# Compressed latents of an attention layer: four passes in the order query 0, key 0, key 1, query 1 in place of query 0, query 1, key 0, key 1

## The chip, the cores and the metric

The kernel runs on one NeuronCore of one Trainium2 chip. TensorE (PE) does the matrix products and the transposes, VectorE (DVE) and ScalarE (ACT) the elementwise work, GpSimd (POOL) a little, and SyncE (SP) issues most of the loads. The metric is the device time of one execution in microseconds (us): 2163.89 us, the median of three runs (2162.13 to 2165.8).

## What is computed

A two-layer encoder over one sequence of 1024 tokens with width 1024, all in float32. Layer 0 is a short gated convolution and a squared-ReLU MLP. Layer 1 is latent attention with 8 heads and a second MLP. The change is at the seam between layer 0 and the attention of layer 1. There the residual stream is normalised, and two modulated versions of it are made: `h`, from which the queries come, and `hkv`, from which the keys and values come. Each is projected to a narrow latent, the latent is normalised, and the key side gives a rotary key as well:

```python
kv_a = hkv @ kv_a_w                                   # 1024 -> 256 + 64
c_kv = rmsnorm(kv_a[..., :KV_LORA], kv_a_norm_g)      # 256 wide
k_pe = apply_rope(kv_a[..., KV_LORA:], cos, sin)      # rotary key, 64 wide
kv = (c_kv @ kv_b_w).reshape(B, S, N_HEADS, QK_NOPE + V_HEAD)
...
q = (rmsnorm(h @ q_a_w[j], q_a_norm_g[j]) @ q_b_w[j])  # 1024 -> 384 -> heads
```

Then come scores, a softmax under a block-causal mask of chunks of 64 tokens, and the weighted values.

## The kernel before

**Products in three parts.** A float32 product is taken as three products of parts: an operand is rounded to a high part by a copy on ACT, and DVE subtracts it from the original, which leaves the low part. `mm` (L154 to L156) then adds low weights by high data, high weights by low data and high by high into the same sum. `up_split` and `split_w` (L159, L160) do this for weights: `uphi` and `uplo` are the parts of one block of 128 weight columns (128x1024). There are three buffers of each, so a fourth block has to wait until the first has been used.

**Tokens in halves.** The seam works on row tiles (`y`) of 128 tokens; tiles 0 to 3 are half 0 and tiles 4 to 7 half 1. A latent pass takes one half (512 tokens) through all weight blocks: three blocks for the query (384 columns), two for the key (256) and one for the rotary key. One block is 8 steps over the width (`KD`) of three products, 24 products of 128x512.

**The operand of a pass.** `h_steps` makes it, in 8 steps: PE transposes the four row tiles of the half into one PSUM tile (L420), ACT scales and shifts it with the modulation into `tt` (L423), DVE casts the high part (L428) and subtracts the low part (L429). There are two such PSUM tiles (`tp`) and two `tt`. The steps are given to a pass as `steps`, and are written between its products. Two operand buffers are there: `hs[0]` (made in the down projection before, with the query's modulation "1m") and `hs[1]`.

**The end of the layer before.** `Seam.tile` closes a row tile: ACT sums its squares (L271) and takes the root (L273), DVE scales it (L327) and adds the residual (L328), ACT stores it and sums the squares of the new residual, and `flush` scales it for the next layer (L311, into `y`). For tile 7, the last, `flush` is called inside `first_latents`, the function that does the products of query 0. Its operand's last step but one comes after tile 4 and its last after tile 5.

**Order of the latents before.** Query 0 (`first_latents`, with the steps of query 1's operand in its third block), query 1 (with the steps of key 0's operand), key 0 and rotary key 0 (with those of key 1), key 1, rotary key 1. `latent` (L1165 to L1187) evicts each block (L1177), squares it (L1178), sums the squares over the partitions by a product with ones (L1181), takes the root (L1182) and the reciprocal (L1183), scales (L1185) and splits (L1186, L1187) into `qaT` or `ckT`. `rotated` (L1189 to L1197) turns the rotary sums with four copies of 32 rows on ACT (L1194). The split weights of q_a stay for both query passes. Then the weights of the first head are split, and the attention begins, with queries, rotary queries and keys of half 1, then of half 0; the values of the first head lie between the first scores.

**What sets the order on an engine.** The program writes the operations; a scheduler of the tile framework merges them into one list for each engine, keeping dependences; the written order binds it only in `pinned` blocks. Inside a pinned block, and from one pinned block to what comes before, an engine keeps the order in which the operations were written. Each engine works through its list in order.

## Time and profile before

| | |
|---|---|
| median of three runs | 2163.89 us (2162.13 to 2165.8) |
| the profiled execution | 2163.67 us |
| its span, first to last instruction | 2161.9 us |
| mean granted TensorE clock | 0.99 |
| PE busy | 2066.3 us (96%) |
| DVE busy | 1541.7 us (71%) |
| ACT busy | 1082.9 us (50%) |
| moved by DMA | 344.47 MB, mean 159 GB/s |

All times inside the execution are counted from the start of its span. A row of a timeline gives the start, the length, the engine, the line of the kernel before, the operation with its output and inputs and their shapes, and in brackets how long the engine stood idle before it and what released it. Neighbours on one engine overlap by some tenths of a us, so that in a dense row of operations the distance of the starts is the cost. Groups give the number, the busy time, the mean length in ns and the idle time before them.

### The profile page before, as it was taken

Reading aid. Unit: us, or ns where it says so; the run is one execution under the profiler, and the core shown is the slowest. Engines: PE = TensorE matmul, PEld = TensorE weight load, DVE = VectorE, ACT = ScalarE, POOL = GpSimd, SP = SyncE. Lnnn points to the kernel's source line nnn. Section 1 sums busy time; section 2 is a strip of 40 time slices with the busy share of each in tenths; the row PEclk is TensorE's granted clock in tenths of the full one; section 3 lists DMA queues with packets and bytes.
Section 4 is the critical chain, followed back from the end, with each engine's and each line's share of the span. In section 5 each row is a group of like instructions: output and inputs, shape, how many; then the busy total and the mean of one; then the engine's idle time right before and its main releaser. Section 6 shows DMA issues by size and latency. Waiting matters only on the chain.

```text
span 2161.9 us, 25072 instructions
## 1 busy us (share of the span) xinstructions
PE 2066.3 (96%) x9438; PEld 1690.4 (78%) x9438; DVE 1541.7 (71%) x2087; ACT 1082.9 (50%) x1533; POOL 5.3 (0%) x13
## 2 busy tenths in 40 slices
PE   4999999899999999999899999989899999999998
PEld 3788878678888788888677888878678888788886
DVE  6777876876765679877688887765875665566577
ACT  4533354745554444455665655564744454544443
POOL 0000000000000000000000000000000000000000
PEclk9999999999999999999999999999999999999999
DMA  7344464254653889656214231053254653774255
GB/s 224 111 146 146 136 207 142 82 180 161 191 183 128 287 291 324 202 171 207 69 60 127 90 100 35 25 169 127 65 187 156 216 180 126 267 248 163 95 175 173
DMA packets 251023, 344.47 MB, mean 159 GB/s; under 512 B 19253, under 2 KB 142482, under 8 KB 250902
## 3 DMA queue, kind: packets, MB, share of 16 engines
q1 hardware_dynamic: 208408, 252.50, 37.2%
q10 hardware_dynamic: 42494, 90.38, 11.3%
q8 instruction: 74, 1.21, 0.2%
q14 instruction: 47, 0.39, 0.1%
HBM read 258.94 MB, written 83.89 MB: 159 GB/s over the span
## 4 chain that ended last, share of the span: by engine, by line
PE 78%; DVE 11%; ACT 6%; DMA 3%; issue 2%; ACTq 0%; SPq 0%; DVEq 0%
PE one L156 42%; PE mm L156 20%; PE tp L156 7%; PE big L156 4%; PE big L1340 2%; ACT junk L271 2%; DVE y L327 1%; PE tp L1366 1%; DVE raw L328 1%; ACT z L1194 1%; DMA aw<-in_ada_w_dram 1%; DMA raw<-hd 1%; PE tp L420 1%; DVE acc L186 1%; DVE av L892 1%
## 5 line engine op out<-in xcount | busy, mean ns | idle before, releaser
L156 PE MATMUL one<-slot,uphi 128*128 128x512 f32 x1224 | 377.6, 389 | 0.0
L156 PEld LDWEIGHTS one<-slot,uphi 128*128 128x128 f32 x1224 | 230.1, 188 | 48.0 <-issue 0.5
L156 PE MATMUL one<-ring,ring 128*128 128x512 f32 x1152 | 262.9, 389 | 2.3 <-DVE ring L160 2.3
L160 DVE TENSOR_TENSOR uplo<-raw,uphi 128x1024 fp32r<-128x1024 f32 x127 | 153.2, 1221 | 143.1 <-ACT uphi L159 143.1
L156 PEld LDWEIGHTS one<-ring,ring 128*128 128x128 f32 x1152 | 215.9, 188 | 48.3 <-ACT ring L159 3.1
L156 PE MATMUL one<-slot,uplo 128*128 128x512 f32 x612 | 240.5, 393 | 8.2 <-DVE y L515 3.8
L160 DVE TENSOR_TENSOR ring<-raw,ring 128x1024 fp32r<-128x1024 f32 x144 | 174.1, 1219 | 53.8 <-ACT ring L159 53.3
L159 ACT ACTIVATE ring<-raw 128x1024 fp32r<-128x1024 f32 x144 | 149.3, 1051 | 111.7 <-DMA raw<-ha 62.9
L159 ACT ACTIVATE uphi<-raw 128x1024 fp32r<-128x1024 f32 x127 | 134.4, 1060 | 120.6 <-PE one L156 80.1
L156 PE MATMUL big<-slot 128*128 128x512 f32 x768 | 179.3, 393 | 6.8 <-DVE slot L160 4.5
L156 PE MATMUL mm<-ring,ring 128*128 128x512 f32 x768 | 184.8, 390 | 1.0 <-DVE ring L160 1.0
L156 PE MATMUL tp<-ring,ring 128*128 128x512 f32 x768 | 183.9, 389 | 0.0
L156 PEld LDWEIGHTS big<-slot 128*128 128x128 f32 x768 | 144.5, 189 | 38.1 <-DVE slot L160 5.2
L159 ACT ACTIVATE ring<-w 128x1024 fp32r<-128x1024 f32 x80 | 84.7, 1059 | 172.9 <-PE tp L156 93.7
L156 PEld LDWEIGHTS mm<-ring,ring 128*128 128x128 f32 x768 | 143.7, 188 | 31.2 <-DVE ring L160 1.7
L156 PEld LDWEIGHTS tp<-ring,ring 128*128 128x128 f32 x768 | 144.1, 188 | 29.8
L160 DVE TENSOR_TENSOR ring<-w,ring 128x1024 fp32r<-128x1024 f32 x80 | 97.6, 1220 | 79.2 <-ACT ring L159 78.5
L156 PEld LDWEIGHTS one<-slot,uplo 128*128 128x128 f32 x612 | 115.1, 188 | 35.9 <-DVE y L515 5.5
L186 DVE SCALAR_TENSOR_TENSOR acc<-raw,csil,acc 128x1024 f32<-128x1024 f32 x88 | 112.4, 1278 | 27.1 <-DMA raw<-in_ada_w_dram 22.0
L513 ACT ACTIVATE y<-one 128x512 f32<-128x512 f32 x66 | 39.0, 591 | 159.5 <-PE one L156 103.0
L156 PE MATMUL mm<-slot,uphi 128*128 128x512 f32 x344 | 108.7, 398 | 9.5 <-DVE slot L385 9.3
L156 PE MATMUL one<-slot,s 128*128 128x512 f32 x468 | 112.8, 390 | 1.1 <-DVE s L160 1.1
(268 smaller groups left out, 3474.7 us busy)
## 6 DMA issues: line engine op xcount, KB each, us to landing
ha<-y ACTq DMA_DIRECT2D x224, 256.0 KB, 3.9
raw<-ha SPq DMA_DIRECT2D x112, 512.0 KB, 4.0
raw<-in_ada_w_dram SPq DMA_DIRECT2D x80, 512.0 KB, 4.0
raw<-in_mlp_up_w_dram SPq DMA_DIRECT2D x70, 512.0 KB, 4.8
w<-in_mlp_down_w_dram SPq DMA_DIRECT2D x48, 512.0 KB, 7.2
raw<-in_mlp_down_w_dram SPq DMA_DIRECT2D x32, 512.0 KB, 4.1
raw<-in_conv_in_w_dram SPq DMA_DIRECT2D x18, 512.0 KB, 4.0
xs<-raw ACTq DMA_DIRECT2D x18, 512.0 KB, 2.6
```

The lines of the kernel that those rows point to most:

```text
L156: nc.tensor.matmul(out_, lhs[a], rhs[b], start=first and i == 0, stop=last and i == 2, skip_group_check=more)
L159: nc.scalar.activation(hi, src, AF.Copy)
L160: nc.vector.tensor_tensor(lo, src, hi.bitcast(F32), op=ALU.subtract)
L186: nc.vector.scalar_tensor_tensor(acc, raw, s, acc, op0=ALU.mult, op1=ALU.add)
L271: nc.scalar.activation(junk, src, AF.Square, accum_out=ss)
L327: nc.vector.scalar_tensor_tensor(y, y, rroot(ss), self.gmb, op0=ALU.mult, op1=ALU.mult)
L328: nc.vector.tensor_tensor(xr, xr, y, op=ALU.add)
L420: nc.tensor.transpose(p_[:, t * P:(t + 1) * P], ys[half * 4 + t][:, k * P:(k + 1) * P], ident)
L513: nc.scalar.activation(dst, x_, AF.Copy)
L892: nc.vector.scalar_tensor_tensor(acc, raw[:, i, :], csil[:, i:i + 1], acc, op0=ALU.mult, op1=ALU.add)
L1194: nc.scalar.activation(y[32 * i:32 * i + 32, :], p_[32 * j:32 * j + 32, :], AF.Copy, scale=scale)
L1340: nc.tensor.matmul(o_, a, m_, start=j == 0, stop=j == 4)
```

## The change

The passes go in the order query 0, key 0, rotary key 0, key 1, rotary key 1, query 1. The steps that are written into them follow: query 0 takes the steps of key 0's operand (half 0, whose row tiles are 0 to 3), key 0 and rotary key 0 those of key 1, and rotary key 1 takes those of query 1. The first block of query 0 does all 8 products of low weights first, then the 8 of high by high, then the 8 with the operand's low parts. The query weights do not stay split: they are loaded and split a second time, three blocks of 512 KB, for query 1. The sine table `stab` goes to a row tile. At the start of the attention both keys come first, then queries and rotary queries of half 0, two of the four blocks of values, queries and rotary queries of half 1; the other two blocks of values lie between the first scores.

```diff
--- before.py
+++ after.py
@@ -560,15 +560,20 @@
         ps_ = []
         for m, w in enumerate(ws):
             p_ = mm_ps() if m else big_ps()[:, :HALF]
+            ps_.append(p_)
+            if m == 0:
+                with pinned():
+                    for a, b in ((1, 0), (0, 0), (0, 1)):
+                        for k in range(KD):
+                            nc.tensor.matmul(p_, w[a][:, k, :], h[b][:, k, :], start=a == 1 and k == 0, stop=b == 1 and k == KD - 1)
+                        seam.flush()
+                continue
             for k in range(KD):
                 with pinned():
                     mm(p_, (w[0][:, k, :], w[1][:, k, :]), (h[0][:, k, :], h[1][:, k, :]), k == 0, k == KD - 1)
-                    if m == 0 and k == 0:
-                        seam.flush()
-                    elif m == 2:
+                    if m == 2:
                         seam.back()
                         seam.front(steps, 1)
-            ps_.append(p_)
         with pinned():
             seam.back()
         return ps_
@@ -1159,7 +1164,7 @@
     ckT = [pp.tile([P, 2, S], F32R, name=f"ckT{i}") for i in range(2)]
     h1 = pool("h1", "right")
     hs = [hq0, tuple(h1.tile([P, KD, HALF], F32R, name=nm("h1")) for _ in range(2))]
-    firsts = first_latents(seam, h_steps(tp, ys, 1, "1m", hs[1]), ws, hs[0])
+    firsts = first_latents(seam, h_steps(tp, ys, 0, "kv", hs[0]), ws, hs[0])
 
     def halves_of(*tiles):
         return [t_[:, i * HALF:(i + 1) * HALF] for t_ in tiles for i in range(2)]
@@ -1213,10 +1218,10 @@
                 ld(rq[:, :, P + i * ROPE:P + (i + 1) * ROPE], w3[:, :, q + NOPE:q + NOPE + ROPE])
         return raw
 
-    def rotary_keys(hf):
+    def rotary_keys(hf, steps=None):
         sl = slice(hf * HALF, (hf + 1) * HALF)
         z, y = halves(row_tile())
-        rotated(up_mm(wk, hk[hf]), hf, 1.0, stab, z, y)
+        rotated(up_mm(wk, hk[hf], steps=steps), hf, 1.0, stab, z, y)
         nc.scalar.activation(kk[0][:, sl], z, AF.Copy)
         nc.vector.tensor_tensor(kk[1][:, sl], z, kk[0][:, sl].bitcast(F32), op=ALU.subtract)
 
@@ -1233,20 +1238,20 @@
     for raw, w in zip(raws_a, cols_of(kv_a_w, 2)):
         ld(raw.rearrange("p (k m) -> p k m", k=KD), w.rearrange("(k p) m -> p k m", p=P))
     latent(hs[0], 0, ws, gq, qaT, firsts=firsts)
-    steps = h_steps(tp, ys, 0, "kv", hk[0])
-    latent(hs[1], 1, ws, gq, qaT, steps)
     ws = [up_split(up, raw.rearrange("p (k m) -> p k m", k=KD)) for raw in raws_a]
     wk = up_weights(up, [kv_a_w[:, KL:KL + ROPE]] * 2)
+    stab = row_tile()
+    ld(stab, consts[:, C_T + S:])
     steps = h_steps(tp, ys, 1, "kv", hk[1])
     latent(hk[0], 0, ws, gk, ckT, steps)
-    stab = raw_tile()
-    ld(stab, consts[:, C_T + S:])
-    raw_kv, raw_q = load_kv_b(0), load_q_b(0)
     rotary_keys(0)
     latent(hk[1], 1, ws, gk, ckT)
+    rotary_keys(1, h_steps(tp, ys, 1, "1m", hs[1]))
+    ws = [up_weights(up, [w]) for w in cols_of(q_a_w[0], 3)]
+    raw_kv, raw_q = load_kv_b(0), load_q_b(0)
+    kw = weights_in_rows(raw_kv.rearrange("p (k m) -> p k m", k=2))
     qw_ = weights_in_rows(raw_q[:, :768].rearrange("p (k m) -> p k m", k=3))
-    kw = weights_in_rows(raw_kv.rearrange("p (k m) -> p k m", k=2))
-    rotary_keys(1)
+    latent(hs[1], 1, ws, gq, qaT)
 
     h1.release()
     h0.release()
@@ -1403,9 +1408,13 @@
 
     K, Q, R, V = {}, {}, {}, {}
     for hf in (1, 0):
+        keys(K, kw, 0, hf)
+    for hf in (0, 1):
         queries(Q, qw_, hf)
         rotary(R, qw_, hf, tp_ps)
-        keys(K, kw, 0, hf)
+        if hf == 0:
+            values(V, kw, 0)
+            values(V, kw, 1)
     before, kw0 = None, kw
     for h in range(H):
         more = h + 1 < H
@@ -1419,15 +1428,13 @@
         if before:
             before.turn(2)
         else:
-            values(V, kw0, 0)
-            values(V, kw0, 1)
+            values(V, kw0, 2)
         end()
         pts[6], end = scores(6, K, Q, r_)
         if before:
             before.turn()
             before.mul(3)
         else:
-            values(V, kw0, 2)
             values(V, kw0, 3)
         end()
         pts[5], end = scores(5, K, Q, r_)
```

All lines from L571 on move down by five and more: L1177 is L1182 in the changed kernel, L1186 is L1191, L1194 is L1199.

**ScalarE, end of query 0.** Before, from the squares of tile 7 (`y_5367`) to the first copy of a transposed operand (`tt`); `lat` is the evicted latent.

```order
L271 ACTIVATE junk_7618,small_7619<-y_5367 128x1024
L273 ACTIVATE small_7621<-small_7619,eps_d 128x1
L311 ACTIVATE y_5366<-raw_7505,small_7623 128x1024
L1177 ACTIVATE lat_7814<-big_7660 128x512
L1178 ACTIVATE sq_7816<-lat_7814 128x512
L329 DMA xs_104<-raw_7507 128x1024
L271 ACTIVATE junk_7631,small_7632<-raw_7507 128x1024
L1177 ACTIVATE lat_7814<-mm_7688 128x512
L273 ACTIVATE small_7634<-small_7632,eps_d 128x1
L1178 ACTIVATE sq_7816<-lat_7814 128x512
L311 ACTIVATE y_5367<-raw_7507,small_7664 128x1024
L423 ACTIVATE tt_7722<-tp_7717,v_6804,v_6800 128x512
```

The same place in the changed kernel; `uphi_7838` and `uphi_7842` are the high parts of the two key weights. The eight `tt` copies stand right behind the last row here.

```order
L159 ACTIVATE uphi_7838<-raw_7810 128x1024
L273 ACTIVATE small_7621<-small_7619,eps_d 128x1
L311 ACTIVATE y_5366<-raw_7505,small_7623 128x1024
L1182 ACTIVATE lat_7814<-big_7660 128x512
L1183 ACTIVATE sq_7816<-lat_7814 128x512
L1182 ACTIVATE lat_7814<-mm_7688 128x512
L329 DMA xs_104<-raw_7507 128x1024
L271 ACTIVATE junk_7631,small_7632<-raw_7507 128x1024
L1183 ACTIVATE sq_7816<-lat_7814 128x512
L273 ACTIVATE small_7634<-small_7632,eps_d 128x1
L159 ACTIVATE uphi_7842<-raw_7811 128x1024
L311 ACTIVATE y_5367<-raw_7507,small_7669 128x1024
```

Two weight splits that stood later are now between the squares of tile 7 and its scaling (`L311`, `y_5367`), and the `tt` copies are behind that scaling as they were.

**ScalarE, rotary key 1.** Before, from the root of key 1's squares: the four rotary copies (`L1194`), the rounded latent (`ckT`), and then the first queries of the attention.

```order
L1182 ACTIVATE sq_8207<-tp_8208,eps_95 128x512
L1194 ACTIVATE y_8281<-mm_8282 32x512 x3
L1186 ACTIVATE ckT_7653<-lat_8206 128x512
L1194 ACTIVATE y_8281<-mm_8282 32x512
L1186 ACTIVATE ckT_7653<-lat_8206 128x512
L1299 ACTIVATE q_8344<-mm_8334 128x512
L159 ACTIVATE qw_8576<-raw_8434 128x3x128
```

In the changed kernel, the same root, the rotary copies, a split of a query weight, the latent, and then the first two copies for the operand of query 1.

```order
L1187 ACTIVATE sq_8030<-tp_8031,eps_95 128x512
L1199 ACTIVATE y_8096<-mm_8097 32x512 x4
L159 ACTIVATE uphi_8217<-raw_8215 128x1024
L1191 ACTIVATE ckT_7653<-lat_8029 128x512 x2
L423 ACTIVATE tt_8106<-tp_8101,v_6804,v_6800 128x512
L423 ACTIVATE tt_8118<-tp_8113,v_6804,v_6800 128x512
L159 ACTIVATE w_8227<-raw_8221 128x1024
L1225 ACTIVATE kk_7651<-y_8096 128x512
L423 ACTIVATE tt_8130<-tp_8125,v_6804,v_6800 128x512
```

The copies `tt_8106` and `tt_8118`, which empty the two PSUM tiles of transposes, stand behind the rotary copies and a weight split.

**TensorE, rotary key 1.** Before, the last products of rotary key 1 (`mm_8282`) and the first of the queries:

```order
L156 MATMUL mm_8282<-h_1085_7658,uplo_8021 128x512
L156 MATMUL mm_8282<-h_1086_7659,uphi_8020 128x512
L156 MATMUL mm_8282<-h_1085_7658,uphi_8020 128x512
L156 MATMUL mm_8282<-h_1085_7658,uplo_8021 128x512
L156 MATMUL mm_8282<-h_1086_7659,uphi_8020 128x512
L156 MATMUL mm_8282<-h_1085_7658,uphi_8020 128x512
L156 MATMUL mm_8334<-qaT_7649,w_8274 128x512
L156 MATMUL mm_8334<-qaT_7650,w_8273 128x512
L156 MATMUL mm_8334<-qaT_7649,w_8273 128x512
```

In the changed kernel the last products of rotary key 1 (`mm_8097`), then the third and fourth set of four transposes for query 1's operand, and then its first product (`mm_8239`):

```order
L156 MATMUL mm_8097<-h_1085_7658,uplo_7850 128x512
L156 MATMUL mm_8097<-h_1086_7659,uphi_7849 128x512
L156 MATMUL mm_8097<-h_1085_7658,uphi_7849 128x512
L420 MATMUL tp_8125<-cs,y_5364 128x128
L420 MATMUL tp_8125<-cs,y_5365 128x128
L420 MATMUL tp_8125<-cs,y_5366 128x128
L420 MATMUL tp_8125<-cs,y_5367 128x128
L420 MATMUL tp_8137<-cs,y_5364 128x128
L420 MATMUL tp_8137<-cs,y_5365 128x128
L420 MATMUL tp_8137<-cs,y_5366 128x128
L420 MATMUL tp_8137<-cs,y_5367 128x128
L156 MATMUL mm_8239<-h_1085_7658,uplo_8206 128x512
```

Two sets of transposes (`tp_8101`, `tp_8113`) lie between the earlier products of rotary key 1; the third and fourth follow it, ahead of any product of query 1.

## The prediction

> **What bounds the kernel now.** I read the page first, then the stretch around the change: the windows of 1026 to 1165 us, the timelines of the three engines there, and the groups by form.
>
> ```profile
> span 2161.9 us, 25072 instructions
> PE 2066.3 (96%) x9438; PEld 1690.4 (78%) x9438; DVE 1541.7 (71%) x2087; ACT 1082.9 (50%) x1533; POOL 5.3 (0%) x13
> PE 78%; DVE 11%; ACT 6%; DMA 3%; issue 2%; ACTq 0%; SPq 0%; DVEq 0%
> ```
>
> TensorE (PE) is busy for 96% of the span and holds 78% of the chain that ended last. So a change that only reorders products can win what PE stands idle where it acts, and lose what new idle time it makes. The windows show where that is:
>
> ```profile
> 1030.00:1035.00 5.00, 2.75 (x11) 1.76 (x10) 1.88 (x4) 4.02 (x8) 0.00 (x0) 1.00 0.53 198
> 1041.00:1048.00 7.00, 1.20 (x7) 0.68 (x5) 3.53 (x5) 5.76 (x10) 0.00 (x0) 0.93 0.19 76
> 1048.00:1054.00 6.00, 6.00 (x21) 4.81 (x21) 2.83 (x6) 2.33 (x3) 0.00 (x0) 0.51 0.01 3
> 1138.00:1142.00 4.00, 3.21 (x9) 2.29 (x8) 3.94 (x6) 1.26 (x2) 0.00 (x0) 0.65 0.46 102
> 1122.18:1164.82 42.64, 38.90 (x195) 31.22 (x193) 40.21 (x66) 26.89 (x48) 0.95 (x1) 0.96 0.46 138
> ```
>
> Columns: length, then busy time of PE, weight loads, VectorE (DVE), ScalarE (ACT), GpSimd, then granted clock. Query 0 has two holes (1030 to 1035, 1041 to 1048), and for six us behind the second the clock is 0.51. The start of attention (last row) is DVE's: busy 40.21 of 42.64. PE's timeline names the waits:
>
> ```profile
> 1033.11 0.50 PE L156 MATMUL big<-h,uplo 128*128 128x512 f32 x1 [1.35 <-ACT h L423]
> 1034.51 0.73 PE L156 MATMUL big<-h,uphi 128*128 128x512 f32 x2 [0.89 <-DVE h L429]
> 1042.22 0.33 PE L420 MATMUL tp<-cs,y 128*128 128x128 f32 x1 [0.62 <-ACT y L311]
> 1047.73 0.48 PE L420 MATMUL tp<-cs,y 128*128 128x128 f32 x1 [5.19 <-ACT y L311]
> 1058.59 0.47 PE L156 MATMUL mm<-h,uplo 128*128 128x512 f32 x1
> 1072.52 0.50 PE L156 MATMUL mm<-h,uplo 128*128 128x512 f32 x1 [1.63 <-ACT lat L1177]
> ```
>
> First 2.24 us for the eighth block of the operand, then 5.81 us for row tile 7, which the second half's transposes read; 1058.59 is where the second pass (query 1) begins. The obvious promise is those 5.81 us and the slow clock behind them, some 3 more, since key 0's operand comes from tiles 0 to 3.
>
> **Term 1, query 0: +0.1 us.** All high parts of the operand are now read in the first eight products. PE meets the eighth block seven products in, waits for the same copy, and restarts at the same 1033.11, with 16 products to go where two were left. The first row below to the second is 48 products, 10.91 us, so 0.227 us each: 16 take 3.6, and the first pass ends near 1037.1 in place of 1035.07.
>
> ```profile
> 1104.55 0.40 PE L156 MATMUL mm<-h,uplo 128*128 128x512 f32 x1
> 1115.46 0.39 PE L156 MATMUL mm<-h,uplo 128*128 128x512 f32 x1
> 1073.68 0.48 PE L156 MATMUL mm<-h,uplo 128*128 128x512 f32 x1
> 1074.81 0.48 PE L156 MATMUL mm<-h,uplo 128*128 128x512 f32 x1
> 1117.80 1.10 PE L1181 MATMUL tp<-sq,ones 128*128 128x512 f32 x2
> 1122.18 2.20 PE L156 MATMUL mm<-qaT,w 128*128 128x512 f32 x9
> ```
>
> Those two us are hidden, for PE has to wait again in the third pass. Its transposes no longer need tile 7, but their buffers do: there are two, and ACT empties them. In the new order all eight copies (tt) still stand behind the scaling of tile 7 (y, L311), and the chain to it has grown by both splits of the key weights. The chain in ACT's and DVE's timelines:
>
> ```profile
> 1039.66 1.04 ACT L271 ACTIVATE junk<-y 128x1024 bf16<-128x1024 f32 x1
> 1046.54 1.14 ACT L311 ACTIVATE y<-raw,small 128x1024 f32<-128x1024 f32 x1
> 1048.25 0.78 ACT L423 ACTIVATE tt<-tp,v,v 128x512 f32<-128x512 f32 x1 [0.57 <-PE tp L420]
> ```
>
> ```profile
> 1041.36 1.28 DVE L327 SCALAR_TENSOR_TENSOR y<-y,small,gmb 128x1024 f32<-128x1024 f32 x1
> 1042.68 1.23 DVE L328 TENSOR_TENSOR raw<-raw,y 128x1024 f32<-128x1024 f32 x1
> ```
>
> The groups by form give what is put in (mean ns of one):
>
> ```profile
> L159 ACT ACTIVATE uphi<-raw 128x1024 fp32r<-128x1024 f32 x3 | 3.2, 1055 | 2.5 <-PE mm L156 2.5
> L423 ACT ACTIVATE tt<-tp,v,v 128x512 f32<-128x512 f32 x24 | 18.6, 778 | 9.4 <-PE tp L420 8.4 <-DVE h L429 0.6 <-PE mm L156 0.3
> L1194 ACT ACTIVATE y<-mm 32x512 f32<-32x512 f32 x8 | 4.7, 590 | 2.9 <-PE mm L156 2.8
> L1186 ACT ACTIVATE ckT<-lat 128x512 fp32r<-128x512 f32 x4 | 2.5, 634 | 1.7 <-DVE lat L1185 1.6
> ```
>
> ```profile
> L160 DVE TENSOR_TENSOR uplo<-raw,uphi 128x1024 fp32r<-128x1024 f32 x3 | 3.5, 1182 | 0.3 <-ACT uphi L159 0.3
> L1183 DVE RECIPROCAL sq<-sq 128x512 f32<-128x512 f32 x4 | 13.4, 3350 | 5.9 <-ACT sq L1182 5.9
> ```
>
> ACT sums tile 7's squares at 1039.66 as before, then splits a key weight (1.06) ahead of the square root. DVE subtracts that split's low part (1.18) ahead of the reciprocal, so its scaling (L327) starts 1.85 late, at 1043.2, and the sum (L328) ends near 1045.75. ACT's eviction of query 0 waits for that scaling; two evictions and one square now stand ahead of the next sum of squares, which starts near 1046.65; then come 1.05 for it, 0.5 for a square, 0.2 for a root and 0.97 for the second split. The L311 of tile 7 starts at 1049.4 in place of 1046.54; with its own time (1.14, the copy starting 0.1 before its end) and the copy's 0.78 the first copy ends at 1051.25, and only then can the third set of transposes go. Left are that set and five steps of three products and a set, 1.13 each (1073.68 to 1074.81), of which a set is 0.45 (less three products of 0.227): 0.45 + 5.65, so the second pass starts at 1057.35 at full clock. The wait before it, 3 to 6 us, is like the 5.81 of now, behind which the clock was 0.51; part of that must be expected. I take 1.3, so 1058.7 against 1058.59: +0.1, from -1.2 (no slow clock) to +1.9 (3 us of it).
>
> **Term 2, the wait at 1072.52: -1.4 us.** It is for the first eviction of that pass, which stood behind one more weight split:
>
> ```profile
> 1070.92 1.06 ACT L159 ACTIVATE uphi<-raw 128x1024 fp32r<-128x1024 f32 x1 [0.39 <-PE mm L156]
> 1071.89 1.07 ACT L1177 ACTIVATE lat<-mm 128x512 f32<-128x512 f32 x2
> ```
>
> ```profile
> 1069.79 1.28 DVE L1187 TENSOR_TENSOR qaT<-lat,qaT 128x512 fp32r<-128x512 f32 x2
> 1101.03 0.42 DVE L428 CAST h<-tt 128x512 fp32r<-128x512 f32 x1
> 1101.48 0.69 DVE L429 TENSOR_TENSOR h<-tt,h 128x512 fp32r<-128x512 f32 x1
> 1102.09 0.42 DVE L428 CAST h<-tt 128x512 fp32r<-128x512 f32 x1
> ```
>
> Now that split is done earlier. The eviction then waits for the tile it writes, free when the first row here ends (1071.07, 12.5 after the pass began), and takes 0.6. PE comes to it after 48 products, one sum by ones (1.10) and two sets of transposes: 12.9. Some 0.25 of 1.63 stays; bounds 0 and -1.6.
>
> **Term 3, rotary key 1 into query 1: +7.5 us.** The transposes for query 1 now begin inside rotary key 1, with no third pass of 24 products to lie beside. Count from rotary key 1's first product (1115.46 now). PE: 24 products 5.44, the ones 1.10, two sets 0.9, so 7.45; then the third set needs the first buffer emptied. ACT first copies the rotary sums, which need the last of those products (four at 0.59, to 9.8), splits a query weight (to 10.8), rounds two latents (1.27, to 12.1), and only then copies the first set (0.78, to 12.9). PE stands still from 7.45 to 12.9. Nothing fills this: query 1's first product needs that operand. Behind it DVE is the bound: a step costs it 1.06 (1101.03 to 1102.09), eight 8.5; between them stand two 128x1024 subtractions (1.14 each), one of 768 columns (0.9) and two rotary ones (0.6 each). So the last low part is there at 25.8, PE has 12 products left (2.7) and the third pass (5.44): 34.0. Without a hole it would be 7.45 + 72 x 0.227 + 6 x 0.45 = 26.5. Bounds: 5.4, if only PE's own hole counts, and 9.0, with a slow clock behind it.
>
> Its other additions cost nothing by themselves: three reloads of 512 KB stand on SP's queue behind the sine table, which waits for row tile 0 until query 0 is over, still some 30 us before their splits.
>
> **Term 4, start of attention: +0.8 us.** As DVE sets this stretch, I count its work. Of 128x512 operations at 0.69, four of the rotary key, two scalings and two low parts of key 1 leave; one sum, three scalings and three low parts of query 1 come, with a whole reciprocal (3.35; now all but 0.8 of it is over by 1122.18). That is -5.5 + 4.8 + 2.55 = +1.9. The ones product of query 1 (1.10), counted in PE's work earlier before, lies beside it: -1.1. Bounds: -3.1, as the keys and values put ahead could take away PE's own waits there (1.7 in the row below) and the slow clock (4 us at 0.65, 1.4 lost), and +3, should DVE then also wait for the weights that SP brings later.
>
> ```profile
> L1340 PE MATMUL big<-k,q 128*128 128x512 f32 x18 | 7.5, 473 | 1.7 <-ACT k L1293 0.9 <-DVE k L1294 0.8
> ```
>
> **Sum.** 0.1 - 1.4 + 7.5 + 0.8 = +7.0 us. Behind 1165 us PE has next to no idle time in which to make this up. The profiled execution took 2163.67 us (1.77 around its span), close to the median of 2163.89, so I forecast 2170.7.
>
> [...] The row of 1048 to 1054 shows half clock behind a wait of 5.8 us. [...]
>
> **The rivals.** [...] (b) Not slower: the hole at 1042 goes altogether, because the copies get past tile 7. PE would do 40 products (9.1) from 1033.11 and eight steps (9.0), and be through at 1051.2, or 1053.2 with some slow clock: 7.4 to 5.4 better, where the sum has +0.1, so -0.5 to +1.5 in all and a time near 2164.2. The point that decides is whether the first tt copy starts before 1046. The written order on ACT speaks against it. (c) Faster: ACT empties the first transposes of query 1 in time, so term 3 falls to nothing, and the start of attention reaches its lower bound: 0.1 - 1.4 - 3.1 = -4.4, or -5.7 with query 0 at full clock, so 2158.0 to 2159.3. For it: those waits are real. Against: ACT's four copies need PE's last rotary product.
>
> **Numbers.** Chances: forecast 0.64, (a) 0.12, (b) 0.12, (c) 0.12. A difference of 0.2% (4.3 us) is about what a measurement of this kernel can tell. Slower by more: most of the forecast (0.55) and (a), 0.67; within: the forecast's low end (0.09), (b) and a little of (c) (0.03), 0.24; faster, the rest of (c), 0.09. All low bounds together give -1.2 - 1.6 + 5.4 - 3.1 = -0.5, all high ones 1.9 + 0 + 9.0 + 3 = +13.9; they will hardly fall on one side, so the range goes from (b)'s low end, 2163.0, to 2176.0, and leaves out (c) and what is above (a).
>
> **What would show it.** Right: tile 7's L311 near 1049.4 and transposes waiting on ACT's tt near 1051; PE idle some 5 us in the middle of rotary key 1's transposes, released by ACT; the 1.63 at the third pass gone. Wrong: tt copies before 1046; no PE wait over 2 us before query 1; attention's first scores reached no later than now.

## The result, and the profile after

The changed kernel takes 2173.36 us (median of five runs, 2172.03 to 2176.8) beside 2162.66 us (2160.9 to 2165.8) for the kernel before: ratio 1.0051, 95% interval 1.0040 to 1.0061. It is slower by 10.7 us, where 7.0 was forecast. Its profiled execution took 2174.26 us. From here on the lines of the changed kernel are five higher than before in all that lies behind query 0 (L1182 for the eviction L1177, L1191 for L1186, L1315 for L1310, L1351 for L1346).

The first lines of its page:

```profile
span 2172.5 us, 25085 instructions
PE 2067.8 (95%) x9438; PEld 1691.6 (78%) x9438; DVE 1544.6 (71%) x2090; ACT 1086.7 (50%) x1536; POOL 5.3 (0%) x13
PE 77%; DVE 11%; ACT 6%; DMA 3%; issue 2%; ACTq 0%; SPq 0%; DVEq 0%
```

PE does the same 9438 products and is busy for 1.5 us more; the span is 10.6 longer. So most of the loss is idle time. PE's timeline, the rows with waits of 0.3 us or more between query 0 and the first softmaxes of the first head (the idle time stands in brackets, with what ended it):

```profile
1032.36 0.75 PE L568 MATMUL big<-h,uplo 128*128 128x512 f32 x1 [4.53 <-ACT h L423]
1049.87 1.12 PE L420 MATMUL tp<-cs,y 128*128 128x128 f32 x4 [3.35 <-ACT tt L423]
1104.29 1.97 PE L420 MATMUL tp<-cs,y 128*128 128x128 f32 x8 [5.40 <-ACT tt L423]
1135.32 0.49 PE L156 MATMUL tp<-qaT,w 128*128 128x512 f32 x1 [0.32 <-ACT qaT L1191]
1144.35 1.69 PE L156 MATMUL mm<-w,ckT 128*128 128x256 f32 x12 [0.93 <-DVE q L1305]
1149.66 0.79 PE L1345 MATMUL big<-kk,r 128*128 128x512 f32 x1 [3.62 <-DVE r L1315]
1162.98 0.50 PE L1345 MATMUL big<-kk,r 128*128 128x512 f32 x1 [0.95 <-ACT p L1351]
1165.22 0.50 PE L1345 MATMUL big<-kk,r 128*128 128x512 f32 x1 [0.31 <-ACT p L1351]
1167.78 0.44 PE L1345 MATMUL big<-kk,r 128*128 128x384 f32 x1 [1.12 <-ACT p L1351]
```

The 7.88 us at query 0 (4.53 + 3.35) stand against 8.05 before (1.35 + 0.89 + 0.62 + 5.19), the wait of 1.63 at 1072.52 has no successor, and the 5.40 in front of query 1's operand is the hole that was forecast. New and not forecast is the 3.62 in front of the first scores.

To see where the loss falls, two stretches are enough: from query 0's first product to the end of the latents, and from there to the first head's first store, which its DMA row gives (16 stores, first and last start):

```profile
L1402 ACTq DMA_DIRECT2D hd<-o x16: 326/326/377, 1170.9 to 1418.6; - x16
```

That is the kernel before; the changed one:

```profile
L1407 ACTq DMA_DIRECT2D hd<-o x16: 326/326/377, 1179.9 to 1427.6; - x16
```

From the first to the last store both take 247.7 us, so nothing is lost or won inside the eight heads after the first store. (A head stores twice, once for each half.) The windows of the two stretches, before (length, then busy PE, weight loads, DVE, ACT, POOL, and the granted clock):

```profile
1026.84:1122.18 95.34, 85.53 (x394) 66.47 (x392) 71.02 (x100) 57.79 (x90) 0.00 (x0) 0.96 0.19 56
1122.18:1170.90 48.72, 44.94 (x230) 36.12 (x228) 44.60 (x78) 30.63 (x57) 0.95 (x1) 0.96 0.41 121
```

and in the changed kernel:

```profile
1026.09:1125.17 99.08, 85.80 (x391) 66.95 (x390) 71.41 (x103) 60.66 (x94) 0.00 (x0) 0.95 0.24 70
1125.17:1179.90 54.73, 46.80 (x230) 37.23 (x228) 46.93 (x77) 30.37 (x55) 0.96 (x1) 0.94 0.36 108
```

The latents take 3.7 us more and the start of attention 6.0 more. The ones product of query 1 (1.10) now lies in the second stretch, so the latents lose 4.8 and attention 4.9. The remaining 0.9 of the 10.6 lies outside: query 0 starts 0.75 earlier, and the part behind the last store is 1.6 longer. The latter is scatter: in the second profiles of the two kernels (runs 11 and 12) that part is 1.2 shorter in the changed one.

### The profile page after: what moved, and what is told of

The parts are those of the page before. It is cut to its first block, busy times and chain, and to the rows that moved or that the text cites. A ratio compares the mean times of both kernels' runs of the same rounds, so it can differ in the third digit from the quotient of the medians.

```text
span 2172.5 us, 25085 instructions
## 1 busy us (share of the span) xinstructions
PE 2067.8 (95%) x9438; PEld 1691.6 (78%) x9438; DVE 1544.6 (71%) x2090; ACT 1086.7 (50%) x1536; POOL 5.3 (0%) x13
## 3 DMA queue, kind: packets, MB, share of 16 engines
q8 instruction: 74, 1.21, 0.2%
## 4 chain that ended last, share of the span: by engine, by line
PE 77%; DVE 11%; ACT 6%; DMA 3%; issue 2%; ACTq 0%; SPq 0%; DVEq 0%
PE one L156 41%; PE mm L156 20%; PE tp L156 7%; PE big L156 4%; PE big L1345 2%; ACT junk L271 2%; DVE y L327 1%; PE tp L1371 1%; DVE raw L328 1%; DMA raw<-hd 1%; DMA aw<-in_ada_w_dram 1%; ACT z L1199 1%; PE tp L420 1%; DVE small L1348 1%; DVE av L897 1%
## 5 line engine op out<-in xcount | busy, mean ns | idle before, releaser
L186 DVE SCALAR_TENSOR_TENSOR acc<-raw,csil,acc 128x1024 f32<-128x1024 f32 x88 | 112.7, 1281 | 23.4 <-DMA raw<-in_ada_w_dram 18.8
```

The source lines that it names most:

```text
L186: nc.vector.scalar_tensor_tensor(acc, raw, s, acc, op0=ALU.mult, op1=ALU.add)
```

## The experiments

Each run was timed five times or more beside the kernel before on the same chip, except the last two, which are single executions. A ratio is to the kernel before; it can differ a little from the ratio of the medians.

**1. The order of query 0's parts undone.**

```diff
-            if m == 0:
-                with pinned():
-                    for a, b in ((1, 0), (0, 0), (0, 1)):
...
                     mm(p_, (w[0][:, k, :], w[1][:, k, :]), (h[0][:, k, :], h[1][:, k, :]), k == 0, k == KD - 1)
-                    if m == 2:
+                    if m == 0 and k == 0:
+                        seam.flush()
+                    elif m == 2:
                         seam.back()
```

> Undoes one part of the change: query 0's products go back to all three kinds for each contraction part (no low parts last); all else is as in the changed kernel. Theory (the order of the parts is worth little, since the pass behind it is held by ScalarE's rounded transposes of tile 7, which stand behind the square pass of L311 in either order): 2173 us, within 1 us of the changed kernel. Rival (TensorE's wait of 4.53 us at query 0 costs its length, and the order of the parts made or filled it): the time moves by 2 us or more, down to 2169 if the wait goes and up to 2176 if the mixed order waits longer.

2176.35 us, ratio 1.0062 (1.0050 to 1.0075). The waits at query 0 are 1.34 + 0.89 + 5.36 = 7.59 us, as long as with the low parts last (7.88). The latents take 99.96 us by its trace (99.08 in the changed kernel). The median is 3.0 us above that of the changed kernel, where the theory had it within 1, but the intervals overlap, so the part order is worth 0 to 3 us, not told apart. What the waits show is that it moves idle time about: 2.23 and then 5.36 us here, 4.53 and then 3.35 with the low parts last.

**2. The rest of the seam issued behind query 0's steps.**

```diff
-                        seam.flush()
...
         with pinned():
             seam.back()
+            seam.flush()
```

> Changes one place: what was held back from the tiles in front of the latents is issued behind query 0's own steps and not ahead of them, so that ScalarE has the rounded transposes of tile 7 ahead of one of the two splits of key weights. Theory (ScalarE's queue sets the start of query 0's second pass): the first rounded transpose starts some 2 us earlier, at 1047 and not 1049, and the time falls by 1 to 2.5 us, to 2171 to 2172. Rival (what holds the pass is the chain of sums of squares and square roots of tile 7 itself): no change, 2173 within 0.5.

2173.7 us, ratio 1.0051 (1.0037 to 1.0066): no change. In its trace PE's two waits that matter are these:

```profile
1046.78 0.66 PE L420 MATMUL tp<-cs,y 128*128 128x128 f32 x4 [1.37 <-ACT tt L423]
1067.52 0.50 PE L156 MATMUL mm<-h,uplo 128*128 128x512 f32 x1 [1.37 <-ACT lat L1182]
```

Query 0 starts at 1025.03 here, so the third transposes go 21.75 us behind it (23.78 in the changed kernel): ACT's order does set that wait, and 2 us of it go. The clock does not fall behind the shorter wait (1.00 from 1046.78 to 1052.55), and so the second pass begins 27.52 us behind query 0, 3.75 us sooner than in the changed kernel (31.27). But the split that was passed over now stands ahead of the first eviction of the next pass: from the second pass to rotary key 1 it takes 35.80 us in place of 33.85, 1.37 of it the wait above. From there to the end of the latents it is 34.76 in place of 33.96, which the next section comes back to. So the latents are 1.0 us shorter (98.08), and the total shows nothing of it.

**3. Query 1's operand made in key 1's second block.**

```diff
-    latent(hk[1], 1, ws, gk, ckT)
-    rotary_keys(1, h_steps(tp, ys, 1, "1m", hs[1]))
+    latent(hk[1], 1, ws, gk, ckT, h_steps(tp, ys, 1, "1m", hs[0]))
+    rotary_keys(1)
...
-    latent(hs[1], 1, ws, gq, qaT)
+    latent(hs[0], 1, ws, gq, qaT)
```

> Query 1's operand is made in a buffer of its own during key 1's second block, and not behind rotary key 1; its second pass follows rotary key 1 as before. Theory (the 5.4 us hole between rotary key 1 and query 1, and VectorE's low parts behind it, are 7.5 us on the path): 2166 to 2168, down by 5.4 to 7.5. Rival 1 (attention's first head starts late by VectorE's and the accumulations' work whatever the latents do): the latents end 5 to 7 us earlier and the first store of the first head only 0 to 3 us earlier; 2171 to 2173. Rival 2 (the slow clock behind the hole was a cost of its own beside the hole): down by more than 8, under 2165.

2168.49 us, ratio 1.0028 (1.0016 to 1.0041). The windows of its two stretches:

```profile
1028.78:1120.62 91.84, 83.78 (x391) 65.86 (x390) 71.47 (x103) 60.45 (x94) 0.00 (x0) 0.96 0.26 76
1120.62:1175.40 54.78, 46.81 (x230) 37.30 (x228) 46.91 (x77) 30.37 (x55) 0.95 (x1) 0.94 0.36 107
```

The latents are 7.24 us shorter, the amount of term 3, and the start of attention takes exactly what it took (54.78 beside 54.73), with the same wait of 3.62 in front of the scores. So by the windows the hole and the part of DVE's work behind it are on the path in full, rival 1 falls, and the loss in attention doesn't hang on when the latents end. In the medians 4.9 us are left of it, half a us less than the theory's low end. (In the profiled execution query 0 started 2.7 us later than in the changed kernel; why is not known.)

**4. The first head without its background accumulations.**

```diff
-        run_bg(5)
+        run_bg(5 if h else 0)
```

> As the changed kernel, but the background accumulations of the modulation sums (L186 on VectorE) are not issued in the first head; they come in the later heads. The same sums are made. Theory (these accumulations stand among the reciprocals and rotary rows of the first head on VectorE, which TensorE waits for at the scores for 3.62 us and then works at a clock of 0.50): the first head's first store comes 3 to 5 us earlier, 2168 to 2170. Rival (VectorE has the room, and what the first head loses is TensorE's clock and the exponentials on ScalarE): within 1 us of 2173. Second rival (the accumulations then pile up in later heads): slower, 2174 to 2177.

2181.09 us, ratio 1.0083 (1.0070 to 1.0096): slower. By its trace 2.2 us of that lie in the first head (56.93 us from the end of the latents to the first store); much of the rest lies in later heads, as the second rival has it. But the edit did not do what it was for. Seven accumulations of L186 lie between 1141 and 1163 us as in the changed kernel, drawn forward from the next head. What did change is PE's list: the next head's keys and queries now stand ahead of the scores and fill the wait for `r`. Then nothing is left between the scores, and PE waits 3.21 and 2.27 us for exponentials. So it says nothing on the accumulations, and it leaves a question for the runs that follow: is the first head short of work to put beside its softmaxes?

**5. The old order at the start of attention, on the new latents.** The third part of the change undone:

```diff
     for hf in (1, 0):
-        keys(K, kw, 0, hf)
-    for hf in (0, 1):
         queries(Q, qw_, hf)
         rotary(R, qw_, hf, tp_ps)
-        if hf == 0:
-            values(V, kw, 0)
-            values(V, kw, 1)
+        keys(K, kw, 0, hf)
...
-            values(V, kw0, 2)
+            values(V, kw0, 0)
+            values(V, kw0, 1)
...
+            values(V, kw0, 2)
             values(V, kw0, 3)
```

> The changed kernel with only the start of attention put back to its old order (queries, rotary rows and keys of half 1, then of half 0; the values between the first scores). Theory A (what the first head loses, 4.9 us, is that query 1's latents are done last: VectorE's reciprocal, scaling and low parts come behind TensorE's last pass whatever follows, and the new order is what hides part of it behind keys, half 0 and values): slower, 2175 to 2179, with a wait of 5 us or more in front of half 1's queries. Theory B (the new order is itself the loss, since it spends the values ahead of the scores, and the old one starts the scores 10 us sooner): faster by 2 to 5 us, 2168 to 2171.

2178.67 us, ratio 1.0080 (1.0067 to 1.0092): clearly slower than the changed kernel, as theory A has it. PE's timeline behind query 1's last product:

```profile
1132.00 1.10 PE L1186 MATMUL tp<-sq,ones 128*128 128x512 f32 x2 [2.16 <-DVE sq L1185]
1138.71 0.79 PE L156 MATMUL mm<-qaT,w 128*128 128x512 f32 x1 [5.62 <-ACT qaT L1191]
```

With query 1 last, half 1's queries wait for the sum of squares, the reciprocal and the scaling: 7.78 us with nothing beside it. The new order hides that behind keys, half 0 and values.

**6. The accumulations held behind the scores.**

```diff
-        run_bg(5)
+        if h:
+            run_bg(5)
...
         pts[5], end = scores(5, K, Q, r_)
+        if not h:
+            with pinned([mybir.EngineType.DVE]):
+                run_bg(5)
```

> The changed kernel with the first head's background accumulations held behind the scores of row tile 5 on VectorE (the run before this one, in which they were left out of the first head's own code, had as many of them in the stretch, drawn forward from the next head). Three accumulations of 1.28 us no longer stand ahead of the rotary rows of half 1; two low parts of values (1.28 together) move ahead instead. Theory (VectorE's queue sets the start of the scores): the rotary rows are done some 2.5 us sooner, TensorE's wait of 3.62 us in front of the scores falls under 1.2, and the time falls by 2 to 4 us, to 2169 to 2171. Rival (TensorE fills the wait with the keys and queries of the next head, and lacks them between the first scores, where each softmax is waited for instead): the wait moves behind the first two row tiles of scores, and the time stays within 1.5 us of 2173 or rises.

2174.35 us, ratio 1.0055 (1.0042 to 1.0067): no gain. The rival is right, and PE's timeline shows it:

```profile
1146.04 1.65 PE L156 MATMUL mm<-ckT,w 128*128 128x512 f32 x6 [0.71 <-DVE v L1329]
1154.75 0.50 PE L1345 MATMUL big<-kk,r 128*128 128x512 f32 x1 [0.67 <-ACT p L1351]
1157.07 0.50 PE L1345 MATMUL big<-kk,r 128*128 128x512 f32 x1 [0.29 <-ACT p L1351]
1160.21 0.50 PE L1345 MATMUL big<-kk,r 128*128 128x512 f32 x1 [1.21 <-ACT p L1351]
1165.07 0.69 PE L1345 MATMUL big<-kk,r 128*128 128x384 f32 x1 [3.43 <-ACT p L1351]
```

The 3.62 in front of the scores is gone. Waits for exponentials of 0.67, 0.29, 1.21 and 3.43 us come instead, 5.60 where they were 0.95, 0.31 and 1.12. In the chain of waits of the changed kernel these accumulations hold 10.8% of the stretch from 1125 to 1182 us; taking them out of the way of the scores was worth nothing all the same.

**7. The order of the parts alone, on the kernel before.** The hunk in `first_latents`, nothing else.

> The kernel before with one part of the change alone: query 0 takes all products of the high parts first and the low parts last. The halves keep their old order. Theory (its wait of 2.24 us for the eighth block only moves behind the square and scaling passes of row tile 7, which end when they did): 2162, within 1 us of the kernel before. Rival (the order of parts is worth the 2 to 3 us by which the run with mixed parts was slower than the changed kernel): 2159 to 2160.

2162.03 us beside 2161.9, ratio 0.9997 (0.9988 to 1.0006): no difference, as the theory has it. Its profiled execution (2159.6 us, span 2157.8) would have told otherwise: the latents take 92.36 us there, 3.0 less than in the first profile of before. The last section comes back to that.

**8. The new order at the start of attention alone, on the kernel before.** The part that run 5 took out, put into the kernel before.

> The kernel before with another part alone: the new order at the start of attention (keys of both halves, then queries and rotary rows of half 0, two values, half 1; values 2 and 3 between the scores). The latents keep their old order, so nothing waits for query 1. Theory A (the loss of the first head comes from query 1 being last): within 1.5 us of the kernel before, 2161 to 2164. Theory B (the new order itself starts the scores later and leaves TensorE nothing to do beside the first softmaxes): slower by 3 to 5 us, 2165 to 2167.

2167.17 us, ratio 1.0022 (1.0013 to 1.0031): slower by 4.8 us by the ratio, 5.3 by the medians. Theory B. Its second stretch and PE's waits in it:

```profile
1119.25:1172.10 52.85, 45.02 (x228) 35.83 (x226) 45.44 (x78) 30.69 (x56) 0.95 (x1) 0.97 0.36 111
```

```profile
1141.36 0.50 PE L1340 MATMUL big<-kk,r 128*128 128x512 f32 x1 [2.60 <-DVE r L1310]
1152.15 0.50 PE L1340 MATMUL big<-kk,r 128*128 128x512 f32 x1 [1.15 <-ACT p L1346]
1154.46 0.50 PE L1340 MATMUL big<-kk,r 128*128 128x512 f32 x1 [0.30 <-ACT p L1346]
1157.27 0.50 PE L1340 MATMUL big<-kk,r 128*128 128x512 f32 x1 [0.89 <-ACT p L1346]
1160.14 0.45 PE L1340 MATMUL big<-kk,r 128*128 128x384 f32 x1 [1.45 <-ACT p L1346]
```

The scores begin 22.1 us behind the end of the latents (13.1 before, 1135.32 less 1122.18; 24.5 in the changed kernel). PE is idle for 7.83 us of the stretch, as in the changed kernel (7.93), and not for 3.78 as before. Here nothing waits for query 1. So the idle time in the first head belongs to the new order itself. All four blocks of values are done ahead of the first score here (24 products from 1129.17, 24 from 1135.53).

**9. Row tiles 3 to 0 first, on run 3.** In the first head the scores of half 0 come ahead of those of half 1, since its queries are ready first (the same sums are made, in another order):

```diff
+        if h == 0:
+            pts[3], end = scores(3, K, Q, r_)
+            values(V, kw0, 2)
+            end()
+            ...
+            pts[7], end = scores(7, K, Q, r_)
+            first.turn(2)
```

> The run with query 1's operand made in key 1's second block (2168.5), and besides, the first head works on row tiles 3 to 0 before 7 to 4, since their queries are there some 10 us before those of half 1; its second half's values close the head. The same sums are made. Theory (the first head's loss is that its scores begin with the row tiles whose queries come last): TensorE's wait of 3.62 us and the slow clock behind it go, the waits on exponentials get the small row tiles as filling, and the time falls by 2 to 5 us, to 2163.5 to 2166.5, near the kernel before. Rival (the end of the head hangs on VectorE's and ScalarE's softmax work of the large row tiles, which now starts later): the wait moves to the end of the head and the time stays at 2167 to 2172.

2175.9 us, ratio 1.0057 (1.0045 to 1.0070): slower than run 3 by some 6 us (by the ratios), and neither the theory nor the rival had that. The scores begin sooner (17.75 us behind the end of the latents, 24.49 in run 3), but the first maximum stands on DVE behind half 1's rotary rows and three accumulations, and PE waits there:

```profile
1149.44 0.58 PE L1345 MATMUL big<-kk,r 128*128 128x256 f32 x1 [8.93 <-ACT p L1351]
```

**10. The same with the accumulations held back as in run 6.**

> The run just above, and besides, the first head's background accumulations are held behind the scores of row tile 5 on VectorE. Theory (VectorE's queue ahead of half 1's rotary rows is what is left): 1 to 2.5 us below the run above. Rival (nothing waits for those rows any more once the small row tiles come first): within 1 us of it, or above it as the accumulations come among the softmaxes.

2167.33 us, ratio 1.0017 (1.0008 to 1.0025): 8.6 us below run 9, far more than the theory's 1 to 2.5; the wait of 8.93 is gone (the longest of those is 1.59). It is below run 3 by 1.2 us in the medians and 2.4 by the ratios, and the intervals overlap. This is the best that was found with the new order of the passes, and it is still slower than the kernel before. Of the 9.1 us between the spans of run 9 and run 3 some 8 lie behind the first head; why was not settled.

**11 and 12. The two kernels profiled once more**, unchanged.

> The kernel before, unchanged, profiled a second time. Theory (waits come from the instruction order and repeat; the slow clock behind a wait repeats too): query 0's start to the second pass again 31.5 to 32.0 us, with waits of 1.35, 0.89 and some 5.2 us and a clock near 0.5 behind the last; end of latents to the first head's first store again 48.5 to 49 us. Rival (whether the clock falls behind a wait differs from execution to execution): the waits repeat within 0.2 us, but the stretch behind them is up to 3 us shorter, as in the run with the parts alone (28.85 us).

> The changed kernel, unchanged, profiled a second time. Theory: query 0's start to the second pass 31 to 31.5 us; rotary key 1's first product to the end of query 1's third pass 33.9 to 34.1 us with the wait of 5.4 us; from there to the first store 54.5 to 55 us with the wait of 3.6 us. Rival as for the run before it: the same waits, and stretches up to 3 us shorter or longer by the clock alone.

Single executions of 2163.08 and 2173.93 us; another single one of the kernel before, beside them, took 2167.87, so single times say little. The second profile of before has the same waits (1.36, 0.89, 0.61, 5.18, then 1.63), but 30.34 us from query 0's start to the second pass in place of 31.75, and 93.90 for the latents in place of 95.34; to the first store it takes 48.69 (48.72). The second profile of the changed kernel repeats all of its stretches: 31.41 (31.27) to the second pass, 99.50 (99.08) for the latents, 54.81 (54.73) to the first store, with waits of 5.40 and 3.58 us. So the waits named here repeat within 0.2 us except for that in front of the third transposes (2.89 and 3.35), and stretches of the kernel before differ by up to 1.4 us.

## Why the prediction was right, and where it failed

With both profiles of each kernel the latents lose 4.7 us (99.3 less 94.6), or 5.8 with the ones product; the first three terms made +6.2. The start of attention loses 6.1 (54.8 less 48.7), or 5.0 without the ones product; the fourth term said +0.8. So the 3.7 us that the forecast missed come from the fourth term, which left its own bounds of -3.1 to +3. The time fell within the range all the same, since the other three came out near their values and the range reaches 5.3 us above the forecast.

**Term 1, query 0, +0.1: right.** From query 0's first product to the second pass it is 31.75 and 30.34 us before, 31.27 and 31.41 after: between -0.5 and +1.1. The chain is the one that was worked out, in ACT's timeline of the changed kernel:

```profile
1047.07 1.04 ACT L159 ACTIVATE uphi<-raw 128x1024 fp32r<-128x1024 f32 x1
1048.02 1.14 ACT L311 ACTIVATE y<-raw,small 128x1024 f32<-128x1024 f32 x1
1049.06 1.43 ACT L423 ACTIVATE tt<-tp,v,v 128x512 f32<-128x512 f32 x2
```

The split of key weights, tile 7's L311 and then the copies, the first at 1049.06, far from the 1046 at which rival (b) would have come in. L311 comes 21.93 us behind query 0's first product, where 22.56 was worked out. Run 2 shows that even with the first copies past tile 7 most of the gain is lost again further on.

**Term 2, -1.4: right in its mechanism.** No idle time is left at the third pass. From the second pass to rotary key 1's first product (1091.21) it is 33.85 us in both profiles of the changed kernel; before, 1058.59 to 1115.46, less query 1's pass of 21.1 (72 products of 0.227, eight sets of 0.455, a ones product), it is 35.77: -1.9, a little beyond the low bound of -1.6.

**Term 3, +7.5: right, with its working.** From rotary key 1's first product (1091.21) to the end of query 1's third pass (1125.17) it takes 33.96 us, 34.24 in the second profile; 34.0 was forecast. ACT's timeline has the queue that was named:

```profile
1098.92 2.39 ACT L1199 ACTIVATE y<-mm 32x512 f32<-32x512 f32 x4 [2.13 <-PE mm L156]
1101.33 1.06 ACT L159 ACTIVATE uphi<-raw 128x1024 fp32r<-128x1024 f32 x1
1102.30 1.13 ACT L1191 ACTIVATE ckT<-lat 128x512 fp32r<-128x512 f32 x2
1103.46 1.45 ACT L423 ACTIVATE tt<-tp,v,v 128x512 f32<-128x512 f32 x2
```

Four rotary copies, a weight split, two latents, and only then the copy that empties the transposes' buffer. Run 3 took the hole away and got the whole 7.2 us back in the latents.

**The clock behind the hole.** The clock did fall behind that hole, and DVE hid what it cost only in part. Windows of the changed kernel and of run 2, and then the weight load (PEld) and the last low part (L429) of the changed kernel:

```profile
1104.29:1107.53 3.24, 3.24 (x12) 2.54 (x13) 3.07 (x6) 2.75 (x4) 0.00 (x0) 0.50 0.00 0
1101.43:1106.53 5.10, 5.10 (x18) 4.11 (x19) 4.93 (x9) 3.53 (x5) 0.00 (x0) 0.50 0.00 0
```

```profile
1116.15 0.69 DVE L429 TENSOR_TENSOR h<-tt,h 128x512 fp32r<-128x512 f32 x1
1116.89 0.19 PEld L156 LDWEIGHTS mm<-h,uphi 128*128 128x128 f32 x1 [0.18 <-DVE h L429]
```

From PE's restart the clock is 0.50 for 3.24 us in the first profile of the changed kernel, for 4.01 in the second and for 5.10 in run 2; the three stretches take 33.96, 34.24 and 34.76 us. In all three the last low part ends 25.6 us behind rotary key 1's first product. In the first profile a weight load waits 0.18 us for it, and 36 products follow: DVE sets the pace, as the prediction had it, and the slow clock is hidden. In the other two PE is still 2 and 4 products behind when that low part is ready, nothing waits for DVE, and the clock costs 0.3 and 0.8 us.

The forecast's 7.5 has no slow clock in it, its bound of 9.0 has. The half clock came in all three profiles, and between nothing and 0.8 us was paid for it.

**Term 4, +0.8: mis-sized, it is +4.9.** The step that failed is the count of DVE's operations as the whole price of the new order, with the keys and values put ahead as a possible gain only. The count itself came out: DVE is busy for 46.93 us of the stretch in place of 44.60, 2.3 more where 1.9 was counted. But the amount of DVE's work is not what sets the stretch: DVE stands idle for 7.80 us of it in place of 4.12. The new order is a loss. PE's timeline in the old order, the waits and the values (`mm<-w,ckT`) between the first scores, which begin at 1135.32:

```profile
1137.16 0.50 PE L1340 MATMUL big<-k,q 128*128 128x512 f32 x1 [0.88 <-ACT k L1293]
1139.15 1.22 PE L1340 MATMUL big<-k,q 128*128 128x512 f32 x2 [0.79 <-DVE k L1294]
1142.30 1.74 PE L156 MATMUL mm<-w,ckT 128*128 128x256 f32 x12
1145.22 3.02 PE L156 MATMUL mm<-w,ckT 128*128 128x256 f32 x24
1157.75 0.44 PE L1340 MATMUL big<-kk,r 128*128 128x384 f32 x1 [0.56 <-ACT p L1346]
```

Three of the four blocks of values lie between the first scores there, and PE does them while DVE and ACT work on the softmaxes. The changed program still writes two blocks between the first scores, but on PE all four are over before the first score at 1149.66 (they start at 1133.31, 1137.99, 1141.83 and 1144.35). Run 8 gives the new order its size, +4.1 us in the stretch and 4.8 by the ratio, with nothing else changed. Of what the changed kernel has beyond that, 54.73 less 52.85, 1.10 is the ones product; the other 0.8 was not traced. So query 1's late reciprocal, on which the term was built, costs at most that in the new order; run 5 shows what it costs in the old one. That the lack of filling work is the reason was argued from these rows and from runs 4 and 6, in which the wait only changes its place: in front of the scores, or between them. It was not shown by a run that gave such work back, and the best try (run 10) got 1.2 to 2.4 us, within the intervals.

**Rivals.** (a) stands for a clock that falls behind each new hole and that PE pays in full. At 3 us, an estimate from the six us at 0.51 behind the wait at query 0 before, it comes to 2174. The time is near that, but no run shows such a price, so that this nearness is luck: the clock did fall, to 0.50, but behind the hole of term 3 it cost 0 to 0.3 us in the two profiles of the changed kernel, and that behind the 3.62 (0.50 from 1149.66 to 1154.66) is mostly hidden too: in run 2, where that stretch had 0.67, the way to the first store was 54.49 us, 0.24 less. (b) and (c) did not come in; (c)'s bound, that the order would take PE's own waits and a slow clock away, is the very point on which the term failed.

## What to carry to other kernels

When products are moved ahead of a chain of waits, ask what the engine will do between the links of that chain afterwards: here three of four blocks of values lay there, and the order that has them done ahead of the scores lost 4.8 us by itself (run 8), though that their place is the reason was argued and not shown. In runs 4 and 6 a wait that was taken away in front of such a chain (3.62 us) came back inside it (3.21 and 2.27 us in run 4, 5.60 in all in run 6), so price a stretch by its whole idle time. And a change in several parts may hold a part that loses on its own and is needed only because of another: here the new start of attention costs 4.8 us on the old passes and saves some 6 on the new ones (ratio 1.0051 with it, 1.0080 without).

## What was not expected of the hardware

How long TensorE worked at the lower clock behind the same wait differed between two executions of the kernel before: some 6 us in one, 3 in the other. The first profile of before, inside its wait of 5.19 us, which ends at 1047.73, and behind it:

```profile
1043.60:1047.00 3.40, 0.00 (x0) 0.00 (x0) 0.80 (x3) 3.09 (x7) 0.00 (x0) 1.00 0.40 157
1047.80:1050.80 3.00, 3.00 (x10) 2.51 (x11) 1.12 (x2) 1.19 (x2) 0.00 (x0) 0.50 0.02 5
1050.80:1053.80 3.00, 3.00 (x11) 2.30 (x11) 1.54 (x3) 1.14 (x2) 0.00 (x0) 0.50 0.00 0
```

The second profile of the same kernel, inside the same wait (5.18 us, it ends at 1047.30) and behind it, and at the place where the first had a clock of 0.65 behind waits of 0.88 and 0.79 us:

```profile
1043.60:1047.00 3.40, 0.00 (x0) 0.00 (x0) 0.86 (x2) 3.12 (x6) 0.00 (x0) 0.50 0.40 157
1047.40:1050.40 3.00, 3.00 (x10) 2.51 (x11) 1.12 (x2) 1.23 (x2) 0.00 (x0) 0.50 0.02 5
1050.40:1053.40 3.00, 3.00 (x21) 2.51 (x20) 2.27 (x5) 1.89 (x3) 0.00 (x0) 1.00 0.00 0
1136.10:1140.10 4.00, 3.21 (x19) 2.52 (x18) 3.94 (x6) 1.26 (x2) 0.00 (x0) 1.00 0.39 100
```

The clock itself is low about as long in both: 0.50 from 1047.0 to 1053.8 in the first, 6.8 us, and in the second the rows at 0.50 reach from 1043.60 to 1050.40. But in the second 3.7 us of that lie inside the wait, where PE has no product to do, and in the first 0.7. At the second place the clock is 0.65 in the one and 1.00 in the other (waits of 0.89 and 0.79 there), and yet the start of attention takes 48.72 and 48.69 us: the 1.4 us that the prediction put on the slow clock there were not on the path.

What sets the clock, and why it fell at another point of the same wait, no run shows.

For reading these profiles it means that a stretch behind a wait is known to no better than 1.4 us from one execution (31.75 and 30.34 us from query 0's start to the second pass), and that a single profile can be kinder than the median, as that of run 7 was (2159.6 us, median 2162.03).
